# Attention units of two query heads, with score rows in pieces of 512 keys

## The chip, the cores and the metric

The kernel runs on one core of a Trainium2 chip. The metric is the device time of one execution in microseconds, taken as the median of three runs. The engines are TensorE (PE, with its weight loads as PEld), VectorE (DVE), ScalarE (ACT), GpSimd (POOL) and the queue SyncE (SP), which issues the transfers. Each engine works its own list of instructions in order, and waits where an instruction needs something that another engine has not finished.

## What is computed

The reference is a backbone of two layers over 2048 latent tokens and 256 context tokens of width 1024. The even layer has two groups of heads side by side, behind one input projection and ahead of one output projection: four heads of a bidirectional gated delta rule ("gdn"), and attention of four query heads over two heads of keys and values (2304 keys, 128 channels). The odd layer is a Conformer convolution module. The part that the change rewrites is the attention:

```python
def grouped_attend(q, k, v):
    bsz, nq = q.shape[:2]
    qg = q.reshape(bsz, nq, B_KV, B_HEADS // B_KV, B_HD)
    s = jnp.einsum('bqhgd,bnhd->bhgqn', qg, k).astype(F32) * (B_HD ** -0.5)
    p = jax.nn.softmax(s, axis=-1).astype(v.dtype)
    o = jnp.einsum('bhgqn,bnhd->bqhgd', p, v)
    return o.reshape(bsz, nq, B_HEADS * B_HD)
...
    k_all = jnp.concatenate([k_l, k_c], axis=1)
    v_all = jnp.concatenate([v_l, v_c], axis=1)
...
    yb_l = ob * jax.nn.silu(zb_l)
    out_l = jnp.concatenate([ya_l, yb_l.astype(ya_l.dtype)], axis=-1) @ w_out
```

The gated delta rule of the other heads runs over chunks. For each chunk it needs the inverse of a unit triangular matrix, and then a chain of small products that carries a state from chunk to chunk, once forward and once backward.

## The kernel before

Every product in float32 precision is made of three: an operand is split into a high part (hi) and a rest (lo), and hi x hi, hi x lo and lo x hi are summed in PSUM. `mm3` (L135 to L137) issues the three, `split` (L145, L146) makes the parts.

*Layer 0, input (`layer0_in`).* The projections write q, k, v, z and the gdn's operands to DRAM. In the last sections the triangular inverses of the gdn run beside projections: `gdn_subst` works by substitution on diagonal blocks of 32 (names sbC and sbT, two tiles of the pool `subst`). It takes five passes, one for each group of chunks. A pass loads its blocks (L836, L838, L839), then alternates 31 multiplications (L846, on DVE while small, on POOL when large) with 31 reductions on DVE (L847), copies (L849, ACT) and stores the inverses (L855). A generator emits the passes 2 to 4 beside the last projection, so the scheduler may let them run on into the next stage.

*Layer 0, mix (`layer0_mix`).* Two generators are merged: `attention` and `gdn_all`, at a ratio of 865 steps to 500. Gdn needs the inverses of the passes as they come: `gdn_inverse` (tiles psq, psw, pst) and `gdn_chain` (pk, py, pq, pn, pa).

The attention before takes 32 units of one head and 256 queries. A unit has two rows of 128 queries. For each row, `scores` makes five blocks of scores (ps_s, four of 512 keys and one of 256), copies them to tiles S of 1024 keys (the rest in S2 of 256) with their maximum (L1049, DVE), and then takes the exponential in place, three instructions a row (L1058, ACT). `attention` goes over the keys of a unit in nine steps of 256: four transposes (pt, L1091), the cast to phi (L1095, ACT), the rest plo (L1096, DVE), and then `pv`: six products with v of 256 moving columns into po (L1119, L1120, L1123). A plan of numbers says how many score blocks of the next unit are issued in each step. `load_kv_part` loads k and v of one kv head; the stage tile kvraw is an S tile, v is cast to vhi (DVE) and vlo (POOL).

*Layer 0, output.* Tokens in groups of 128 are multiplied by the output weight (ps_out), normed and added to the residual x, whose tiles (x1) are loaded ahead.

The order on each engine is not written by hand: a scheduler with its own timing model sets it from the order in which the generators emit, and from the dependences. Memory is part of these. Pools are stacks that grow from the left or from the right end of SBUF. A pool opened with `reuse_waits="tile"` may use addresses that an earlier, closed pool had, and each of its tiles then waits until the last use of the tiles that lie under it is done.

Of the kernel before, what the change touches and what calls it, by code (L numbers as in the profile page):

```python
# [8 lines left out]
F32 = mybir.dt.float32  # L9
# [22 lines left out]
GDN_STEPS = 500  # L32

# [73 lines left out]
class Build:  # L107
# [82 lines left out]
    def ada_start(self, layer, conds, half, raws, pspool, ap, st):  # L190
        """Scale and shift columns {cond: (A[128,4], B[128,4])} of four channel tiles."""
# [43 lines left out]
    def make_hT(self, xs, A, B, hi, lo, st, tp, cts=range(KT), bufs=3):  # L235
        """xs: token tiles [128,1024] scaled by rstd; writes hi/lo [128 ch, 8, n*128]."""
# [12 lines left out]
    @staticmethod  # L249
    def pipe(gens):  # L250
        """Starts one generator per tick, then each older one takes a step, newest first. A generator
        that is given more than once takes a single step each time."""
# [11 lines left out]
    def rotate(pools):  # L264
        """Allocator over four buffers of the first pool and two of the second, in turn."""
# [9 lines left out]
    def ahead(self, gen, offset, steps=2):  # L275
        """gen, its first steps with a scheduling priority that lies `offset` instructions earlier."""
        for _ in range(steps):
            with self.tc.high_priority(offset):
                next(gen)
            yield  # L280
        yield from gen

    def layer0_in(self):
        tc, nc = self.tc, self.nc
        with ExitStack() as es:
# [67 lines left out]
            with tc.tile_pool(name="stB", bufs=2, reuse_waits="tile") as st:  # L353
# [25 lines left out]
                self.pipe([late])  # L379
            with tc.tile_pool(name="stZ", bufs=2, reuse_waits="tile") as st:  # L380
                self.sub = em.enter_context(tc.tile_pool(name="subst", bufs=1, side="right", reuse_waits="tile"))
# [49 lines left out]
    def load_w(self, src, c0, n, vec=False):  # L431
        """Weight columns [1024, n] as hi/lo half tiles of four k tiles each."""
# [286 lines left out]
    # gated delta rule, chunks of 128 tokens, four heads at a time: first the decayed products of all  # L719
    # chunks and the inverses of their diagonal blocks of 32, then both directions' chains, where the  # L720
    # chain of a chunk runs beside the completion of the next one's inverse and the output of the last
# [95 lines left out]
    def gdn_subst(self, n, chunks):  # L817
        """Inverses of the unit triangular diagonal blocks of 32 of one group of chunks for each direction, by
# [695 lines left out]
```

## Time and profile before

| | |
|---|---|
| median of 3 runs | 2692.19 us (2688.54 to 2692.4) |
| profiled execution | span 2690.4 us, 1.8 us below the median |
| PE busy | 2595.6 us, 96% |
| DVE busy | 2027.2 us, 75% |
| ACT busy | 1357.0 us, 50% |
| POOL busy | 1427.6 us, 53% |
| attention stage | 882 to 1815 us of the span |
| first and last product with v | 912.9 and 1814.7 us |
| first and last reduction of the substitution | 671.0 and 1166.4 us |

In the rows of the profile a tile is written out<-in, with the buffer numbers left out, and "x" gives a count. Times are microseconds from the start of the span, or ns where the text says so. Busy time of PE holds waits as well where matmuls are pipelined, so what an operation costs on PE is read from the distance of two starts or from a window's sum.

### The profile page before, as it was taken

What the parts mean: (1) busy time and instruction counts of PE and PEld (TensorE: products, weight loads), DVE (VectorE), ACT (ScalarE), POOL (GpSimd) and SP (SyncE); (2) the same over time, 40 slices, a digit from 0 to 9 for tenths busy, and PEclk for the clock granted to TensorE, in tenths of its full rate; (3) what the DMA queues carried; (4) which work ended last, traced back from release to release, by engine and by line L of the source; (5) the groups of instructions that cost most, each with busy time, mean ns of one, the idle gap of its engine ahead of it and who ended that gap; (6) DMA issues with size and microseconds to landing.
All of it is one profiled execution on the core that took longest, in us unless ns stands there. A gap on an engine that the chain in (4) does not pass through costs nothing. (4 is left out here: it accounts for less than half of the span.)

```text
span 2690.4 us, 44112 instructions
## 1 busy us (share of the span) xinstructions
PE 2595.6 (96%) x15784; PEld 2235.1 (83%) x15784; DVE 2027.2 (75%) x4048; ACT 1357.0 (50%) x2617; POOL 1427.6 (53%) x1172
## 2 busy tenths in 40 slices
PE   7999999998899899999999999999999999999988
PEld 5888887998788688888888889888888888887867
DVE  8576667776975778776676667656379999997985
ACT  7454465223232555555555555544356767665332
POOL 3344343667776645431243332302169999997764
PEclk9999999999999999999999999999999999999999
DMA  8133334335556654444544433324411211116442
GB/s 308 50 103 101 116 118 130 111 114 147 178 170 199 167 116 109 130 115 120 148 124 122 117 103 97 112 85 135 155 49 40 71 57 62 55 59 202 159 155 98
DMA packets 372731, 323.28 MB, mean 120 GB/s; under 512 B 74784, under 2 KB 301600, under 8 KB 372512
## 3 DMA queue, kind: packets, MB, share of 16 engines
q1 hardware_dynamic: 372512, 320.46, 39.6%
q8 instruction: 125, 2.05, 0.3%
q14 instruction: 94, 0.77, 0.1%
HBM read 216.05 MB, written 104.33 MB: 119 GB/s over the span
## 5 line engine op out<-in xcount | busy, mean ns | idle before, releaser
L1392 POOL TENSOR_TENSOR ac<-ac,pr 128x512 f32<-128x512 f32 x288 | 379.3, 1340 | 22.1 <-ACT ac L1388 10.5
L1384 DVE SCALAR_TENSOR_TENSOR pc<-u,hw,pc 128x1024 f32<-128x1024 f32 x320 | 389.3, 1279 | 2.0 <-ACT pc L1382 0.7
L1095 ACT CAST phi<-pt 128x512 fp32r<-128x512 f32 x288 | 166.6, 586 | 217.5 <-PE pt L1091 207.3
L1391 ACT ACTIVATE pr<-u,hw 128x512 f32<-128x512 f32 x288 | 205.9, 722 | 124.1 <-POOL ac L1392 122.7
L1096 DVE TENSOR_TENSOR plo<-pt,phi 128x512 fp32r<-128x512 f32 x288 | 195.9, 685 | 84.1 <-ACT phi L1095 82.5
L1049 DVE TENSOR_SCALAR_CACHE_REDUCE S<-ps_s 128x512 f32<-128x512 f32 (+1 forms) x320 | 198.9, 631 | 63.3 <-PE ps_s L137 41.5
L135 PE MATMUL ps_b<-w_hi,hhi 128*128 128x256 f32 (+1 forms) x800 | 231.9, 292 | 7.3 <-DVE xn L563 5.8
L136 PE MATMUL ps_b<-w_lo,hhi 128*128 128x256 f32 (+1 forms) x800 | 228.4, 287 | 0.1
L137 PE MATMUL ps_b<-w_hi,hlo 128*128 128x256 f32 (+1 forms) x800 | 227.1, 289 | 0.6 <-POOL hlo L146 0.6
L135 PE MATMUL ps_out<-wohi,yhi 128*128 128x512 f32 x512 | 204.3, 399 | 2.2 <-DVE yhi L145 2.2
L137 PE MATMUL ps_out<-wohi,ylo 128*128 128x512 f32 x512 | 201.6, 395 | 0.6 <-DVE ylo L146 0.6
L136 PE MATMUL ps_out<-wolo,yhi 128*128 128x512 f32 x512 | 202.0, 395 | 0.0
L1058 ACT ACTIVATE S<-S,m 128x1024 f32<-128x1024 f32 (+1 forms) x192 | 177.9, 931 | 36.5 <-DVE m L1055 36.3
L846 POOL TENSOR_TENSOR sbT<-sbC 128x169 f32<-128x169 f32 (+18 forms) x76 | 122.1, 1607 | 103.9 <-DVE sbC L847 79.5
L1091 PE MATMUL pt<-ident,S 128*128 128x128 f32 x1152 | 175.5, 274 | 0.9 <-DVE plo L1096 0.9
L1119 PE MATMUL po<-phi,vhi 128*128 128x256 f32 x576 | 170.1, 317 | 3.8 <-ACT phi L1095 3.2
L135 PE MATMUL ps_a<-hhi,w_hi 128*128 128x512 f32 (+1 forms) x448 | 171.3, 382 | 0.0
L136 PE MATMUL ps_a<-hlo,w_hi 128*128 128x512 f32 (+1 forms) x448 | 170.8, 381 | 0.0
L137 PE MATMUL ps_a<-hhi,w_lo 128*128 128x512 f32 (+1 forms) x448 | 170.3, 380 | 0.2 <-POOL w_lo L146 0.2
L474 DVE SCALAR_TENSOR_TENSOR acc<-ub,cols,acc 128x512 f32<-128x512 f32 (+1 forms) x168 | 138.7, 834 | 33.8 <-POOL acc L472 32.0
L135 PEld LDWEIGHTS ps_b<-w_hi,hhi 128*128 128x128 f32 x800 | 153.9, 193 | 10.0 <-issue 4.8
L136 PEld LDWEIGHTS ps_b<-w_lo,hhi 128*128 128x128 f32 x800 | 154.0, 193 | 1.6 <-DVE w_lo L146 0.6
(323 smaller groups left out, 7699.2 us busy)
## 6 DMA issues: line engine op xcount, KB each, us to landing
raw_ada<-in_ada_w_dram SPq DMA_DIRECT2D x48, 512.0 KB
x<-in_x_dram SPq DMA_DIRECT2D x32, 512.0 KB
kq<-d_kT SPq DMA_DIRECT2D x54, 256.0 KB
raw_w<-in_ev_w_in_dram SPq DMA_DIRECT2D x26, 512.0 KB
kq<-d_qT SPq DMA_DIRECT2D x48, 256.0 KB
raw_w<-in_od_w_in_dram SPq DMA_DIRECT2D x24, 512.0 KB
d_nt<-ntA SPq DMA_DIRECT2D x36, 256.0 KB
nt<-d_nt SPq DMA_DIRECT2D x36, 256.0 KB
```

The costliest lines, as they stand in the source:

```text
L135: self.nc.tensor.matmul(ps, lhsT=lh, rhs=rh, start=(a == 0), stop=False)
L136: self.nc.tensor.matmul(ps, lhsT=lh, rhs=rl, start=False, stop=False)
L137: self.nc.tensor.matmul(ps, lhsT=ll, rhs=rh, start=False, stop=(a == n - 1))
L1049: nc.vector.tensor_scalar(out=S[g][:, k0:k0 + w], in0=ps[:, :w], scalar1=1.0, scalar2=None, op0=ALU.mult, op1=ALU.max, accum_out=mx[:, b:b ...
L1058: nc.scalar.activation(S[g], S[g], AF.Exp, bias=m, scale=scale, accum_out=l[:, g:g + 1])
L1091: nc.tensor.transpose(pt[:, e, a * P:(a + 1) * P], S[a][k0 // 1024][:, k0 % 1024:k0 % 1024 + P], self.ident)
L1095: nc.scalar.copy(hi, pt)
L1096: nc.vector.tensor_tensor(out=lo, in0=pt, in1=hi.bitcast(F32), op=ALU.subtract)
L1119: nc.tensor.matmul(po, lhsT=vhi[:, ks], rhs=hi[:, e, :], start=(k == 0), stop=False)
L1384: nc.vector.scalar_tensor_tensor(out=pc, in0=s(j), scalar=w(j), in1=pc, op0=ALU.mult, op1=ALU.add)
L1391: nc.scalar.mul(pr, s(j), w(j))
L1392: nc.gpsimd.tensor_tensor(out=ac, in0=ac, in1=pr, op=ALU.add)
```

## The change

A unit now is two heads of one kv head with 256 queries, four rows of 128; there are 16. Products have 512 moving columns, three to a step of 128 keys, with 18 steps. The score tiles are pieces of 512 keys (S_BUFS 20) and 256 keys (S2_BUFS 6), so a row has five exponentials. k and v are loaded in pieces of 512. The tiles qr, qhi, qlo and ya have one buffer instead of two and are twice as wide. The pool `subst` is opened on the left side, ahead of stZ and for the whole of `layer0_in`; before it was opened on the right side inside stZ, for the whole of the mix. Comments are removed, which is left out here.

```diff
+S_BUFS = 20
+S2_BUFS = 6
...
+            self.sub = es.enter_context(tc.tile_pool(name="subst", bufs=1, reuse_waits="tile"))
             with tc.tile_pool(name="stZ", bufs=2, reuse_waits="tile") as st:
-                self.sub = em.enter_context(tc.tile_pool(name="subst", bufs=1, side="right", reuse_waits="tile"))
                 with tc.tile_pool(name="prod", bufs=2, side="right", reuse_waits="tile") as gp:
                     prod = self.all_products(gp, self.tp)
...
-                stage = lambda w: self.ap.tile([P, w], F32, tag="S" if w > 256 else "S2", name="kvraw", bufs=7 if w > 256 else 4)
+                stage = lambda w: self.ap.tile([P, w], F32, tag="S" if w > 256 else "S2", name="kvraw", bufs=S_BUFS if w > 256 else S2_BUFS)
...
-        for k0, w in ((0, 1024), (1024, 1024), (2048, 256)):
+        for k0 in range(0, T + TC, 512):
+            w = min(512, T + TC - k0)
...
-    def scores(self, kv, h, qp, kvt):
-        """Yields after each of ten score blocks; the last value is the unit's state."""
+    def scores(self, kv, qp, kvt):
+
         nc, ap = self.nc, self.ap
         scale = float(P) ** -0.5
         khi, klo = kvt[0], kvt[1]
-        qr = ap.tile([P, 256], F32, tag="qr", name="qr", bufs=2)
-        nc.sync.dma_start(qr, self.d_bq[h, :, qp * 256:(qp + 1) * 256])
-        sz = ap.tile([P, 256], F32, tag="sz", name="sz", bufs=2)
-        nc.sync.dma_start(sz, self.d_szb[h, :, qp * 256:(qp + 1) * 256])
-        qhi = ap.tile([P, 256], F32R, tag="qhi", name="qhi", bufs=2)
-        qlo = ap.tile([P, 256], F32R, tag="qlo", name="qlo", bufs=2)
+        hs, ts = slice(2 * kv, 2 * kv + 2), slice(qp * 256, (qp + 1) * 256)
+        qr = ap.tile([P, 2, 256], F32, tag="qr", name="qr", bufs=1)
+        nc.sync.dma_start(qr, self.d_bq[hs, :, ts].rearrange("h p t -> p h t"))
+        sz = ap.tile([P, 2, 256], F32, tag="sz", name="sz", bufs=2)
+        nc.sync.dma_start(sz, self.d_szb[hs, :, ts].rearrange("h p t -> p h t"))
+        qhi = ap.tile([P, 2, 256], F32R, tag="qhi", name="qhi", bufs=1)
+        qlo = ap.tile([P, 2, 256], F32R, tag="qlo", name="qlo", bufs=1)
         self.split(qhi, qlo, qr)
-        st = {"S": [], "r": [], "sz": sz, "h": h, "qp": qp, "kv": kvt}
-        for a in range(2):
-            S = [None] * 3
+        st = {"S": [], "r": [], "sz": sz, "kv": kv, "qp": qp, "kvt": kvt}
+        for e, a in ((0, 0), (0, 1), (1, 0), (1, 1)):
+            S = []
             mx = ap.tile([P, 5], F32, tag="mx", name="mx")
             qs = slice(a * P, (a + 1) * P)
-            for b, (g, k0, w) in enumerate(self.KB):
-                if S[g] is None:
-                    S[g] = (ap.tile([P, 1024], F32, tag="S", name="S", bufs=7) if g < 2
-                            else ap.tile([P, 256], F32, tag="S2", name="S2", bufs=4))
+            for b in range(5):
+                w = 512 if b < 4 else 256
+                S.append(ap.tile([P, 512], F32, tag="S", name="S", bufs=S_BUFS) if b < 4
+                         else ap.tile([P, 256], F32, tag="S2", name="S2", bufs=S2_BUFS))
                 ps = self.ps_s.tile([P, 512], F32, tag="s", name="ps_s")
-                ks = slice(g * 1024 + k0, g * 1024 + k0 + w)
-                self.mm3(ps[:, :w], [(qhi[:, qs], qlo[:, qs], khi[:, ks], klo[:, ks])])
-                nc.vector.tensor_scalar(out=S[g][:, k0:k0 + w], in0=ps[:, :w], scalar1=1.0, scalar2=None,
+                ks = slice(b * 512, b * 512 + w)
+                self.mm3(ps[:, :w], [(qhi[:, e, qs], qlo[:, e, qs], khi[:, ks], klo[:, ks])])
+                nc.vector.tensor_scalar(out=S[b], in0=ps[:, :w], scalar1=1.0, scalar2=None,
                                         op0=ALU.mult, op1=ALU.max, accum_out=mx[:, b:b + 1])
                 if b < 4:
                     yield
             m = ap.tile([P, 1], F32, tag="m", name="m")
             nc.vector.reduce_max(m, mx, axis=AX.X)
             nc.vector.tensor_scalar(out=m, in0=m, scalar1=-scale, scalar2=None, op0=ALU.mult)
-            l = ap.tile([P, 3], F32, tag="l", name="l")
-            for g in range(3):
+            l = ap.tile([P, 5], F32, tag="l", name="l")
+            for g in range(5):
                 nc.scalar.activation(S[g], S[g], AF.Exp, bias=m, scale=scale, accum_out=l[:, g:g + 1])
-            ri = ap.tile([P, 1], F32, tag=f"ri{a}", name=f"ri{a}")
+            ri = ap.tile([P, 1], F32, tag=f"ri{e}{a}", name=f"ri{e}{a}")
             nc.vector.reduce_sum(ri, l, axis=AX.X)
             nc.vector.reciprocal(ri, ri)
             st["S"].append(S)
@@ -1065,16 +1067,14 @@
 
     def attention(self):
         nc, ap = self.nc, self.ap
-        units = [(kv, 2 * kv + hh, qp) for kv in range(KV) for qp in range(T // 256) for hh in range(2)]
-        gen = None
+        units = [(kv, qp) for kv in range(KV) for qp in range(T // 256)]
+        plan = (2, 1, 1, 1) * 4 + (0, 0)
+
+        def start(u):
+            return self.scores(*units[u], self.load_kv(units[u][0]))
+
+        gen = start(0)
         cur = None
-        plan = (2, 1, 2, 1, 2, 1, 1, 0, 0)
-
-        def start(u):
-            kv = units[u][0]
-            return self.scores(*units[u], self.load_kv(kv))
-
-        gen = start(0)
         for cur in gen:
             yield
         pend = None
@@ -1082,60 +1082,58 @@
             gen = start(u + 1) if u + 1 < len(units) else None
             nxt = None
             po = None
-            S, vhi, vlo = cur["S"], cur["kv"][2], cur["kv"][3]
-            for kp in range(NTA // 2):
-                pt = self.ps_t.tile([P, 2, 256], F32, tag="t", name="pt")
-                for e in range(2):
-                    for a in range(2):
-                        k0 = (2 * kp + e) * P
-                        nc.tensor.transpose(pt[:, e, a * P:(a + 1) * P], S[a][k0 // 1024][:, k0 % 1024:k0 % 1024 + P],
-                                            self.ident)
-                hi = ap.tile([P, 2, 256], F32R, tag="phi", name="phi", bufs=2)
-                lo = ap.tile([P, 2, 256], F32R, tag="plo", name="plo", bufs=2)
+            for k in range(NTA):
+                pt = self.ps_t.tile([P, 512], F32, tag="t", name="pt")
+                k0 = k * P
+                for a in range(4):
+                    nc.tensor.transpose(pt[:, a * P:(a + 1) * P], cur["S"][a][k0 // 512][:, k0 % 512:k0 % 512 + P],
+                                        self.ident)
+                hi = ap.tile([P, 512], F32R, tag="phi", name="phi", bufs=2)
+                lo = ap.tile([P, 512], F32R, tag="plo", name="plo", bufs=2)
                 nc.scalar.copy(hi, pt)
                 nc.vector.tensor_tensor(out=lo, in0=pt, in1=hi.bitcast(F32), op=ALU.subtract)
                 yield
                 if gen is not None:
-                    for _ in range(plan[kp]):
+                    for _ in range(plan[k]):
                         nxt = next(gen)
                     yield
                 if pend is not None:
                     pend()
                     yield
-                if kp == 0:
-                    po = self.ps_o.tile([P, 256], F32, tag="o", name="po")
-                pend = self.pv(po, vhi, vlo, hi, lo, kp, cur)
+                if k == 0:
+                    po = self.ps_o.tile([P, 512], F32, tag="o", name="po")
+                pend = self.pv(po, hi, lo, k, cur)
             cur = nxt
         pend()
         yield
 
-    def pv(self, po, vhi, vlo, hi, lo, kp, st):
+    def pv(self, po, hi, lo, k, st):
         nc, ap = self.nc, self.ap
+        vhi, vlo = st["kvt"][2:]
 
         def emit():
-            for e in range(2):
-                k = 2 * kp + e
-                ks = slice(k * P, (k + 1) * P)
-                nc.tensor.matmul(po, lhsT=vhi[:, ks], rhs=hi[:, e, :], start=(k == 0), stop=False)
-                nc.tensor.matmul(po, lhsT=vlo[:, ks], rhs=hi[:, e, :], start=False, stop=False)
-            for e in range(2):
-                k = 2 * kp + e
-                nc.tensor.matmul(po, lhsT=vhi[:, k * P:(k + 1) * P], rhs=lo[:, e, :], start=False, stop=(k == NTA - 1))
-            if kp == NTA // 2 - 2:
-                pr = self.ps_t.tile([P, 256], F32, tag="t", name="pr")
-                for a in range(2):
+            ks = slice(k * P, (k + 1) * P)
+            nc.tensor.matmul(po, lhsT=vhi[:, ks], rhs=hi, start=(k == 0), stop=False)
+            nc.tensor.matmul(po, lhsT=vlo[:, ks], rhs=hi, start=False, stop=False)
+            nc.tensor.matmul(po, lhsT=vhi[:, ks], rhs=lo, start=False, stop=(k == NTA - 1))
+            szf = st["sz"].rearrange("p h t -> p (h t)")
+            if k == NTA - 2:
+                pr = self.ps_t.tile([P, 512], F32, tag="t", name="pr")
+                for a in range(4):
                     nc.tensor.transpose(pr[:, a * P:(a + 1) * P], st["r"][a].to_broadcast([P, P]), self.ident)
-                nc.vector.tensor_tensor(out=st["sz"], in0=pr, in1=st["sz"], op=ALU.mult)
-            if kp == NTA // 2 - 1:
-                y = ap.tile([P, 256], F32, tag="ya", name="ya")
-                nc.vector.scalar_tensor_tensor(out=y, in0=po, scalar=0.5, in1=st["sz"], op0=ALU.mult, op1=ALU.mult)
-                nc.sync.dma_start(self.d_y[H + st["h"], :, st["qp"] * 256:(st["qp"] + 1) * 256], y)
+                nc.vector.tensor_tensor(out=szf, in0=pr, in1=szf, op=ALU.mult)
+            if k == NTA - 1:
+                y = ap.tile([P, 2, 256], F32, tag="ya", name="ya", bufs=1)
+                nc.vector.scalar_tensor_tensor(out=y.rearrange("p h t -> p (h t)"), in0=po, scalar=0.5, in1=szf,
+                                               op0=ALU.mult, op1=ALU.mult)
+                h0 = H + 2 * st["kv"]
+                nc.sync.dma_start(self.d_y[h0:h0 + 2, :, st["qp"] * 256:(st["qp"] + 1) * 256].rearrange("h p t -> p h t"), y)
 
         return emit
```

Three places where the order of the engines changes. A row is a line, an instruction, its tiles, its shape, and a count where rows alike follow each other.

First DVE, where v of the first kv head is cast (vhi<-kvraw). sbC<-sbT is a reduction of the substitution, whose last in the program has the shape 128x31; S,mx<-ps_s copies a score block; qz, r, o and sso belong to the gdn. Before:

```order
L847 TENSOR_REDUCE sbC<-sbT 128x16
L1049 TENSOR_SCALAR S,mx<-ps_s 128x512 x2
L1049 TENSOR_SCALAR S_10400,mx<-ps_s 128x256
L145 CAST vhi<-kvraw 128x1024 x2
L145 CAST vhi<-kvraw 128x256
L898 COPY qz_32_10298<-psq 32x4x32 x2
L1054 TENSOR_REDUCE m<-mx 128x1
L847 TENSOR_REDUCE sbC<-sbT 128x17
```

After:

```order
L849 TENSOR_REDUCE sbC<-sbT 128x30
L900 COPY qz_64_10313<-psq 64x256
L963 TENSOR_TENSOR S_16252<-S_16252,pn 128x512
L963 TENSOR_TENSOR S_16276<-S_16276,pn 128x512
L849 TENSOR_REDUCE sbC<-sbT 128x31
L971 TENSOR_TENSOR o<-o,pa 128x512 x2
L900 COPY qz_32_10307<-psq 32x4x32 x2
L900 COPY qz_32_10311<-psq 32x4x32 x2
L936 SCALAR_TENSOR_TENSOR r<-pk,negc,vt 128x128 x8
L987 TENSOR_REDUCE sso<-o_16438 128x4
L988 TENSOR_SCALAR sso<-sso 128x4
L147 CAST vhi<-kvraw 128x512 x4
```

The casts of v stood in the middle of the third pass of the substitution, and stand behind the last reduction of the fifth. On PE the first product with v moves with them: it was instruction 5101, 97 behind the first score matmul at 5004, and is 6105, 1101 behind it.

Then PE, where the last units of the attention meet the output projection (ps_out). Before, in one of the last units:

```order
L1123 MATMUL po<-plo,vhi 128x256 x2
L135 MATMUL ps_s<-khi,qhi 128x512
L136 MATMUL ps_s<-klo,qhi 128x512
L137 MATMUL ps_s<-khi,qlo 128x512
L1091 MATMUL pt<-ident,S 128x128 x4
L135 MATMUL ps_out<-wohi_21445,yhi 128x512
L136 MATMUL ps_out<-wolo_21446,yhi 128x512
L135 MATMUL ps_out<-wohi_21469,yhi 128x512
L136 MATMUL ps_out<-wolo_21470,yhi 128x512
L1119 MATMUL po<-phi,vhi 128x256
```

After, at the end of the last unit (pr are the transposes of the row sums):

```order
L1123 MATMUL pr<-ident,ri_20230 128x128
L1123 MATMUL pr<-ident,ri_20321 128x128
L1116 MATMUL po<-phi,vhi 128x512
L1117 MATMUL po<-phi,vlo 128x512
L1118 MATMUL po<-plo,vhi 128x512
L137 MATMUL ps_out<-wohi_20645,yhi 128x512
L138 MATMUL ps_out<-wolo_20646,yhi 128x512
L137 MATMUL ps_out<-wohi_20669,yhi 128x512
```

265 matmuls of ps_out stood among the attention's by the trace; now the first stands behind the last product with v.

Last ACT, in the part of the attention after the gdn, from the end of a unit (its last ten casts phi) into the next. S,l<-S,m are exponentials of the pieces of one row: four of 512 and one of 256. After:

```order
L1093 CAST phi<-pt 128x512 x10
L1060 ACTIVATE S,l<-S,m 128x512 x4
L1060 ACTIVATE S_14431,l<-S_14431,m 128x256
L1060 ACTIVATE S,l<-S,m 128x512 x4
L1060 ACTIVATE S_14574,l<-S_14574,m 128x256
L1093 CAST phi<-pt 128x512 x2
L1060 ACTIVATE S,l<-S,m 128x512 x4
L1060 ACTIVATE S_14813,l<-S_14813,m 128x256
L1093 CAST phi<-pt 128x512 x4
```

The exponentials of two whole rows stand between the last cast of a unit and the first of the next, at every one of the 15 boundaries (13 and 15 exponentials at two of them); before there were none to three at such a place.

More of the change, by code (lines that the diff above doesn't have):

```diff
@@ L998, in gdn_final @@
         yield
-    KB = [(0, 0, 512), (0, 512, 512), (1, 0, 512), (1, 512, 512), (2, 0, 256)]
     def load_kv(self, kv):
```

## The prediction

> **What bounds the kernel now.** The page first: TensorE is the busy engine.
>
> ```profile
> span 2690.4 us, 44112 instructions
> PE 2595.6 (96%) x15784; PEld 2235.1 (83%) x15784; DVE 2027.2 (75%) x4048; ACT 1357.0 (50%) x2617; POOL 1427.6 (53%) x1172
> ```
>
> Then the table by windows, cut at the stage that the change touches: 882 us (first scores) to 1815 us (last product with v). Columns: window, its length, busy time (count) of PE, PEld, DVE, ACT, POOL, then granted clock, DMA share, GB/s.
>
> ```profile
> 882.00:1150.00 268.00, 256.16 (x1986) 222.15 (x1985) 214.28 (x603) 146.32 (x318) 141.88 (x120) 0.98 0.51 132
> 1150.00:1655.00 505.00, 502.34 (x3937) 447.21 (x3936) 346.06 (x975) 277.11 (x626) 158.71 (x146) 1.00 0.42 115
> 1660.00:1680.00 20.00, 19.47 (x141) 17.68 (x140) 14.04 (x44) 12.21 (x26) 7.21 (x7) 1.00 0.42 139
> 1680.00:1700.00 20.00, 17.25 (x116) 15.27 (x115) 13.14 (x41) 15.30 (x28) 9.55 (x5) 0.97 0.54 161
> 1700.00:1720.00 20.00, 19.98 (x128) 18.04 (x127) 16.28 (x43) 15.18 (x26) 9.56 (x4) 0.94 0.45 132
> 1720.00:1815.00 95.00, 95.00 (x552) 83.37 (x552) 51.93 (x117) 40.11 (x79) 5.00 (x10) 1.00 0.24 79
> ```
>
> PE is full in all but the first and the fourth, so here a transfer or a DVE operation costs only if PE runs out of work. The same windows for tile po (products with v), then pk (one step of the gdn chain), then ps_out (the output projection of layer 0):
>
> ```profile
> 1150.00:1655.00 505.00, 178.93 (x958) 134.13 (x956) 7.61 (x18) 1.00 0.42 115
> 1660.00:1680.00 20.00, 9.62 (x55) 7.94 (x56) 0.42 (x1) 1.00 0.42 139
> 1680.00:1700.00 20.00, 9.06 (x50) 7.42 (x51) 0.42 (x1) 0.97 0.54 161
> 1700.00:1720.00 20.00, 9.53 (x52) 7.95 (x50) 0.42 (x1) 0.94 0.45 132
> ...
> 882.00:1150.00 268.00, 11.72 (x80) 10.47 (x81) 11.18 (x40) 0.98 0.51 132
> 1150.00:1655.00 505.00, 28.23 (x192) 25.43 (x192) 27.19 (x96) 1.00 0.42 115
> ...
> 1700.00:1720.00 20.00, 2.99 (x12) 2.28 (x13) 0.00 (x0) 0.00 (x0) 0.94 0.45 132
> 1720.00:1815.00 95.00, 62.44 (x253) 46.13 (x252) 13.31 (x20) 7.25 (x21) 1.00 0.24 79
> ```
>
> Three streams share PE until 1815: attention, gdn, and 265 matmuls of ps_out. I price them per record. Attention without gdn, its scores and transposes included, costs (20 + 20 - 12 x 0.23)/(55 + 52) = 0.35 us per po record in the third and fifth windows (0.36 and 0.33 apart; 0.40 in the fourth). So 1728 products stand for 605 us. In 1150 to 1655 the rest is gdn: (505 - 958 x 0.35)/192 = 0.88 per pk record, 240 us for 272. The 265 of ps_out are 61. That is 906 of 933 us; 12 of the rest are idle in the first window.
>
> **The products.** 1728 matmuls of 256 columns become 864 of 512. Pitches, start to start, from the timeline of PE:
>
> ```profile
> 882.88 0.39 PE L136 MATMUL ps_s<-klo,qhi 128*128 128x512 f32 x1
> 883.11 0.39 PE L137 MATMUL ps_s<-khi,qlo 128*128 128x512 f32 x1
> ...
> 1225.06 0.28 PE L1120 MATMUL po<-phi,vlo 128*128 128x256 f32 x1
> 1225.17 0.28 PE L1119 MATMUL po<-phi,vhi 128*128 128x256 f32 x1
> ...
> 1370.93 0.82 PE L1091 MATMUL pt<-ident,S 128*128 128x128 f32 x6
> ```
>
> 0.23 against 0.1175 (0.11 and 0.12 alternate): 203.0 us becomes 198.7, a gain of 4.3 us. The Trainium skill ("TensorE: Matmul & The Clock Gate", section "Back-to-back issue gap") gives columns over 2.4 GHz plus 2.5 ns: 109 and 216 ns, which is an estimate of 2 us saved. The rows lie above both, so I keep 4.3. Transposes (six in 0.82 us, 0.11 each when the last one's 0.27 is taken off) and score matmuls keep their number.
>
> **Score rows in pieces.** Per row four exps of 512 replace two of 1024:
>
> ```profile
> L1058 ACT ACTIVATE S<-S,m 128x1024 f32<-128x1024 f32 x128 | 146.4, 1147 | 36.5 <-DVE m L1055 36.3
> L1058 ACT ACTIVATE S<-S,m 128x256 f32<-128x256 f32 x64 | 31.9, 498 | 0.0
> L1095 ACT CAST phi<-pt 128x512 fp32r<-128x512 f32 x288 | 166.6, 586 | 217.5 <-PE pt L1091 207.3
> L1096 DVE TENSOR_TENSOR plo<-pt,phi 128x512 fp32r<-128x512 f32 x288 | 195.9, 685 | 84.1 <-ACT phi L1095 82.5
> ```
>
> On the line between the two widths 512 columns take about 0.71 us (an estimate from these rows; 0.50 and 1.15 are its ends). 256 x 0.71 - 146.4 is 36 us more on ACT, and each exp brings an accumulator read. ACT is 55% busy in the second window and its casts wait for PE (207.3 us), so the total hides. Where the exps stand does not: a unit now has four rows and the pool S2 six buffers, so the last pieces of the next unit's third and fourth rows wait for this unit's last transposes. In the order on ACT ten exps stand between each unit's last phi and the next one's first; before, none to three. That chain is phi 0.59 + plo 0.69 + exps 8 x 0.71 + 2 x 0.50 = 6.7 + phi 0.59 = 8.5 us; PE has six products (1.4), eight score blocks of three matmuls (six of 512 and two of 256 columns, 4.8) and twelve transposes (1.3) there, 7.5. Gdn fills the first boundaries; for ten I take 1 us each, +10, with ends 0 and 60 (6 us each, if the score blocks must wait for DVE too).
>
> **The moved pool.** This decides. The tiles sbC and sbT of the substitution move from the right side, inside stZ, to the left before it; in the program as built they then share addresses with vhi and vlo of kv head 0 (sbT 190016 to 194112, vhi 184256 to 193472), and a pool that reuses memory waits for its last user. Before they shared none:
>
> ```profile
> L1119 PE MATMUL po<-phi,vhi x576: 274/283/561, 912.9 to 1814.3; 128*128 128x256 f32 x192
> L145 DVE CAST vhi<-kvraw x6: 679/1192/2464, 894.8 to 1370.1; 128x1024 fp32r<-128x1024 f32 x4, 128x256 fp32r<-128x256 f32 x2
> L146 POOL TENSOR_TENSOR vlo<-kvraw,vhi x6: 734/2391/2818, 896.0 to 1375.8; 128x1024 fp32r<-128x1024 f32 x4, 128x256 fp32r<-128x256 f32 x2
> ```
>
> v was cast at 895 and the first product ran at 912.9, long before the substitution ended. Its five passes end in the copies L849 (the first at 757):
>
> ```profile
> 848.70 2.12 ACT L849 COPY sbT<-sbC 128x1024 f32<-128x1024 f32 x1 [4.90 <-DVE sbC L847]
> ...
> 969.47 2.01 ACT L849 COPY sbT<-sbC 128x1024 f32<-128x1024 f32 x1
> ...
> 1065.06 2.08 ACT L849 COPY sbT<-sbC 128x1024 f32<-128x1024 f32 x1 [1.05 <-DVE sbC L847]
> ...
> 1167.60 2.05 ACT L849 COPY sbT<-sbC 128x1024 f32<-128x1024 f32 x1 [1.13 <-DVE sbC L847]
> ...
> L847 DVE TENSOR_REDUCE sbC<-sbT x155: 136/414/1156, 671.0 to 1166.4; 128x1 f32<-128x1 f32 x4, 128x2 f32<-128x4 f32 x4, 128x3 f32<-128x9 f32 x4, 128x4 f32<-128x16 f32 x4
> L846 POOL TENSOR_TENSOR sbT<-sbC x76: 637/1565/3030, 786.5 to 1162.9; 128x169 f32<-128x169 f32 x4, 128x196 f32<-128x196 f32 x4, 128x225 f32<-128x225 f32 x4, 128x256 f32<-128x256 f32 x4
> ```
>
> The lengths are 121, 96 and 103 us. The third pass lost 12 us between two groups of its loads, with v's loads among what stood there on SP; these now stand behind:
>
> ```profile
> 858.48 1.96 SPq L836 DMA_DIRECT2D sbT<-d_nt  x4
> ...
> 870.46 2.42 SPq L836 DMA_DIRECT2D sbT<-d_nt  x4
> ...
> 1174.65 1.81 SPq L855 DMA_DIRECT2D d_w<-sbC  x4
> ```
>
> Its own work bounds a pass below: 19 POOL multiplies at 1.57 and 31 reductions at 0.41, alternating, are 43 us, with loads, small multiplies, copies and stores some 66. Without products fewer plo stand on DVE between its steps, but more gdn operations on DVE and POOL; I take 105, 94 and 93. The last copy then starts at 848.7 + 292 = 1141, its store ends 8 us after (1174.65 + 1.81 - 1167.60 = 8.9 in the row), and v is cast: first product at about 1150. Its ends: 1069 and 1185 (lengths as before, plus stores and casts); 1069 is set by PE, as the next lines show, since three passes of 66 would end sooner, at 1056.
>
> Until then the order on PE holds 96 of the 136 pk matmuls (71% of gdn, 170 us; the trace has two records of each) and 81 of 960 score matmuls (17 us): 187 us of work in 268, so 81 us idle. From 1150 on: 29% of gdn, 70 us; attention 605 - 4 - 17 = 584; boundaries 10; the second head's v (casts around 1370, vlo 2.4 us each) with less gdn to cover it, 6 (ends 0 and 12). The sum is 670: attention ends at 1820.
>
> **What it covered.** The first residual tile of layer 0's output (x1) shared addresses with the substitution before, and shares them now with klo, which the last scores use. The order on PE has no ps_out before the last po; before there were 265. So 61 us follow alone, and about 3 us of start: 1820 + 64 = 1884 where the kernel before stood at 1815. That is +69; behind it nothing changes. From the profiled span 2690.4 it gives 2759, and the median lies 1.8 above that span: **2761 us**. DMA issues of the larger q, sz and ya are half as many and twice as large; q is split for 512 columns at once, DVE is 69% busy in the second window and does that beside PE: nothing.
>
> **The rivals.**
>
> *The substitution runs much faster alone.* The loss is gone when the first product comes 69 us earlier, at 1081, so when a pass takes 74 us: 848.7 + 3 x 74 + 9. Shorter ones gain no more than PE's own 187 us allow, a first product at 1069 and 2680 us. For it: attention was beside every pass after the second. Against: the second pass, mostly without attention, still took 848.7 - 757 = 92 us. Chance 0.08, half of it below 2687 and half on no change.
>
> *Attention alone is slower than I price it.* The fourth window shows 0.40 per record while ACT was 15.30 of 20 us busy. At 0.40 the attention costs 86 us more, and gdn by the same division 0.63 instead of 0.88, 20 us less at the end: +66, 2827. With boundaries of 6 us it goes the same way. Chance 0.12.
>
> *PE runs at half speed while it waits.* After an idle time the pitch was not 0.23:
>
> ```profile
> 890.91 0.77 PE L135 MATMUL ps_s<-khi,qhi 128*128 128x512 f32 x1 [6.72 <-DVE S L1049]
> 891.48 0.63 PE L136 MATMUL ps_s<-klo,qhi 128*128 128x512 f32 x1
> 891.91 0.63 PE L137 MATMUL ps_s<-khi,qlo 128*128 128x512 f32 x1
> ```
>
> 891.48 to 891.91 is 0.43. If the gaps before the first product keep PE in that state, its 187 us there become up to 374 in 268, and the first product slips by up to 106: up to 2867. If only gaps of several us do it, the 80 us of slack hide it. The Trainium skill has this rule (same page, section "Why this matters for your kernels"): a gap of over about 3 us brings the array back to half rate. The row agrees after 6.7 us; none here shows many small gaps. Chance 0.06.
>
> *The wait is not there.* Then only the products (-4) and the boundaries (0 to 10) count, and 2688 to 2698 follows. The order speaks against it: v's casts stand behind the last reduction on DVE. Chance 0.02.
>
> **The numbers.** The forecast, first product between 1105 and 1185, has 0.72: 2715 to 2800. With the second rival and part of the third the range is 2705 to 2830. A measurement here tells about 0.2%, 5 us, from no change. Faster 0.04; same 0.04 and the last rival, 0.06; slower 0.90.
>
> **What would show it.** First product near 1150 and v's casts right behind the last sbC reduction; PE busy about 0.7 from 890 to then; last product near 1820 with no ps_out before; products at a pitch of 0.23; ACT casts waiting for exps at unit boundaries. Wrong, if the substitution ends before 1080, if PE stays full until then, or if the last product comes after 1880.

## The result, and the profile after

The changed kernel takes 2787.69 us (median of four runs, 2784.1 to 2796.48) against 2692.3 before, a ratio of 1.0362 [1.0345, 1.0379]: 95 us slower, where 2761 was forecast, with a range to 2830. Its profiled execution is the slowest of the four, 104.3 us longer in its span than the one before. The first lines of its page:

```profile
span 2794.7 us, 42560 instructions
PE 2612.8 (93%) x14920; PEld 2188.2 (78%) x14920; DVE 2045.9 (73%) x3992; ACT 1395.4 (50%) x2875; POOL 1423.4 (51%) x1178
```

PE has 864 matmuls less and is busy 17 us longer, in a span of which it fills 93% and not 96%. The windows show where (columns as before), then the same for pk:

```profile
882.00:1150.00 268.00, 221.22 (x1957) 193.34 (x1956) 159.01 (x424) 112.93 (x308) 188.56 (x173) 0.92 0.79 217
1162.00:1400.00 238.00, 232.94 (x1586) 192.40 (x1587) 162.88 (x439) 139.67 (x360) 96.27 (x90) 0.98 0.39 113
1400.00:1600.00 200.00, 178.55 (x920) 140.03 (x918) 139.06 (x374) 117.41 (x276) 31.71 (x18) 0.93 0.17 52
1600.00:1820.00 220.00, 208.51 (x1132) 166.01 (x1130) 161.37 (x462) 137.18 (x341) 0.00 (x0) 1.00 0.09 26
...
882.00:1150.00 268.00, 24.77 (x176) 22.33 (x176) 24.09 (x88) 0.92 0.79 217
1162.00:1400.00 238.00, 11.50 (x80) 10.63 (x80) 11.19 (x40) 0.98 0.39 113
```

Before 1150 PE works on gdn (176 of its 272 pk records, 80 before) and on little else, the first unit's scores, and idles 47 us; after 1400, where POOL and the DMA fall quiet, it works on attention alone and idles again. The tile v and the ends of the substitution's passes, from the view by tile and the timeline of ACT, with DVE's and SP's rows at the turning point:

```profile
L1116 PE MATMUL po<-phi,vhi x288: 389/476/793, 1162.3 to 1848.7; 128*128 128x512 f32 x144
L147 DVE CAST vhi<-kvraw x10: 419/1370/1524, 1161.8 to 1554.2; 128x512 fp32r<-128x512 f32 x8, 128x256 fp32r<-128x256 f32 x2
...
857.69 2.12 ACT L851 COPY sbT<-sbC 128x1024 f32<-128x1024 f32 x1 [4.84 <-DVE sbC L849]
955.76 1.96 ACT L851 COPY sbT<-sbC 128x1024 f32<-128x1024 f32 x1 [3.60 <-DVE sbC L849]
1054.18 1.99 ACT L851 COPY sbT<-sbC 128x1024 f32<-128x1024 f32 x1
1151.12 2.01 ACT L851 COPY sbT<-sbC 128x1024 f32<-128x1024 f32 x1 [1.54 <-DVE sbC L849]
...
1158.18 1.81 SPq L857 DMA_DIRECT2D d_w<-sbC  x4
...
1161.78 2.20 DVE L147 CAST vhi<-kvraw 128x512 fp32r<-128x512 f32 x3 [4.56 <-DMA d_w<-sbC]
```

v's casts wait for the last store of the substitution (released by d_w<-sbC), and the first product with v follows at 1162.3, where it stood at 912.9.

How PE's time is spent from the first score matmul to the last product, added up from the traces (start of a matmul to the start of the next; idle is the time from a matmul's end to the next start; waits inside the pitch count to the stream), all in us:

| kernel | first score | first product | last product | attention | gdn | ps_out | idle | from last product to the end |
|---|---|---|---|---|---|---|---|---|
| before | 882.6 | 912.9 | 1814.7 | 599.7 | 253.2 | 61.4 | 17.8 | 875.7 |
| changed | 891.7 | 1162.3 | 1849.3 | 591.6 | 271.9 | 0 | 94.0 | 945.4 |
| b_left | 884.4 | 1175.4 | 1875.1 | 578.1 | 269.2 | 49.1 | 94.2 | 883.2 |
| b_pad | 883.5 | 914.6 | 1752.4 | 602.0 | 248.6 | 0 | 18.4 | 937.1 |
| r16 | 879.9 | 924.2 | 1806.1 | 612.9 | 262.0 | 0 | 51.3 | 940.0 |
| r20g | 883.2 | 928.4 | 1783.2 | 606.4 | 259.2 | 0 | 34.4 | 939.4 |
| s18 | 887.0 | 1183.8 | 1936.2 | 586.4 | 271.0 | 66.5 | 125.4 | 876.8 |

Changed against before: 76 us more idle, 19 more in gdn, 8 less in attention, 9 later at the first score, and ps_out, which leaves the stage (-61) and comes behind it (+70): 104.

### The profile page after: what moved, and what is told of

It is laid out like the page before. It is cut to its first block, busy times and chain, and to the rows that moved or that the text cites. A ratio compares the mean times of both kernels' runs of the same rounds, so it can differ in the third digit from the quotient of the medians.

```text
span 2794.7 us, 42560 instructions
## 1 busy us (share of the span) xinstructions
PE 2612.8 (93%) x14920; PEld 2188.2 (78%) x14920; DVE 2045.9 (73%) x3992; ACT 1395.4 (50%) x2875; POOL 1423.4 (51%) x1178
## 5 line engine op out<-in xcount | busy, mean ns | idle before, releaser
L1060 ACT ACTIVATE S<-S,m 128x512 f32<-128x512 f32 (+1 forms) x320 | 213.2, 669 | 32.5 <-DVE m L1057 30.2
L151 POOL TENSOR_TENSOR rsp<-msp,mhalf 128x1 f32<-128x1 f32 x32 | 19.0, 594 | 405.7 <-DVE msp L1217 405.7
L1089 PE MATMUL pt<-ident,S 128*128 128x128 f32 x1152 | 181.7, 277 | 9.1 <-ACT S L1060 9.1
L1089 PEld LDWEIGHTS pt<-ident,S 128*128 128x128 f32 x1152 | 146.7, 143 | 45.8 <-ACT S L1060 10.4
L137 PE MATMUL ps_s<-khi,qhi 128*128 128x512 f32 (+1 forms) x320 | 139.4, 436 | 25.0 <-DVE S L1051 23.6
```

What stands on the lines that cost most here:

```text
L137: self.nc.tensor.matmul(ps, lhsT=lh, rhs=rh, start=(a == 0), stop=False)
L1060: nc.scalar.activation(S[g], S[g], AF.Exp, bias=m, scale=scale, accum_out=l[:, g:g + 1])
L1089: nc.tensor.transpose(pt[:, a * P:(a + 1) * P], cur["S"][a][k0 // 512][:, k0 % 512:k0 % 512 + P], self.ident)
```

## The experiments

Two theories after the result. **Pool**: sharing addresses with the substitution holds v back, and that idle time is the loss. **Units**: the rewritten units with their order of scores and exps lose the time themselves.

**b_left: the pool alone.**

```diff
--- before
+            self.sub = es.enter_context(tc.tile_pool(name="subst", bufs=1, reuse_waits="tile"))
             with tc.tile_pool(name="stZ", bufs=2, reuse_waits="tile") as st:
-                self.sub = em.enter_context(tc.tile_pool(name="subst", bufs=1, side="right", reuse_waits="tile"))
```

> The kernel before, with one edit: the pool of the substitution (sbC, sbT) is opened on the left, as in the changed kernel; units, score pieces and buffers stay. If the pool's place carries the loss: v of kv head 0 waits for the end of the substitution, first product with v near 1155 us instead of 913, PE busy about 0.7 until then, and some 84 us more minus what ps_out fills later (211 of its matmuls still stand ahead of the last product), so 2755 to 2780 us. If the loss lies in the new units and score pieces: first product near 913 and 2692 us, within 5.

2768.95 us, ratio 1.0287 [1.0259, 1.0315]. With the old units and score pieces the first product comes at 1175.4, and 78 us are lost. The idle time is in sum that of the changed kernel (94 us), but not in the same places: 81 us of it lie ahead of the first product and 13 behind it, against 51 and 43 in the changed kernel. A window ahead of the first product shows how little PE has to do, and at what granted clock (0.77):

```profile
1050.00:1150.00 100.00, 53.61 (x490) 48.25 (x489) 41.41 (x103) 29.25 (x74) 63.45 (x56) 0.77 0.59 156
```

**b_pad: the left side without the shared addresses.**

```diff
--- b_left
+            pad = pool("pad", 1, side="right")
+            pad.tile([P, 4192], F32, name="pad")
             self.vv = pool("vv", 1, side="right")
```

> As b_left (kernel before, pool of the substitution on the left), with 16768 bytes left empty between k and v, so that v of kv head 0 lies below the substitution's tiles. The score tiles then reach down onto the output stage's work tiles, and no ps_out stands ahead of the last product (211 in b_left, 264 before). If sharing addresses with v is what costs: first product back near 913 us, and 2690 to 2705 us, since PE has hardly an idle time that ps_out could fill. If the left side costs for another reason: about 2769, as b_left. If ps_out behind the last product is a loss of its own: 2750.

2693.39 us, ratio 1.0006 [0.9992, 1.0020]. The rows of v in b_left, then in b_pad:

```profile
L145 DVE CAST vhi<-kvraw x6: 685/693/2445, 1174.6 to 1551.9; 128x1024 fp32r<-128x1024 f32 x4, 128x256 fp32r<-128x256 f32 x2
...
L1121 PE MATMUL po<-phi,vhi x576: 274/283/389, 914.6 to 1751.8; 128*128 128x256 f32 x192
L145 DVE CAST vhi<-kvraw x6: 282/688/2460, 875.6 to 1369.4; 128x1024 fp32r<-128x1024 f32 x4, 128x256 fp32r<-128x256 f32 x2
```

The pool is still on the left; v only lies elsewhere, and everything is back. It also settles ps_out: none stands ahead of the last product here, the stage is 63 us shorter and what follows 61 us longer. Its place is no loss while PE is full.

**r16 and r20g: the new units alone.** Both put the pool back on the right in the changed kernel, and pay the 8 KB in different places.

```diff
--- changed (r16)
-S_BUFS = 20
+S_BUFS = 16
-            self.sub = es.enter_context(tc.tile_pool(name="subst", bufs=1, reuse_waits="tile"))
             with tc.tile_pool(name="stZ", bufs=2, reuse_waits="tile") as st:
+                self.sub = em.enter_context(tc.tile_pool(name="subst", bufs=1, side="right", reuse_waits="tile"))
--- changed (r20g): the same move of the pool, S_BUFS stays 20
-        kq = self.load_kq(c, gp, 4)
+        kq = self.load_kq(c, gp, 3)
-            at = gp.tile([P, H, P], F32, tag="at", name="at", bufs=4)
+            at = gp.tile([P, H, P], F32, tag="at", name="at", bufs=3)
-        o = gp.tile([P, H, P], F32, tag="o", name="o", bufs=4) if lat else None
+        o = gp.tile([P, H, P], F32, tag="o", name="o", bufs=3) if lat else None
```

> The changed kernel with the pool of the substitution back on the right side (needs 8 KB: S_BUFS 16 instead of 20, so a unit's score pieces have no spare buffers). If the pool's place carries the loss: first product near 915 us, and the 84 us that PE lost before it are back: about 2704 us (2690 to 2720); ps_out still stands behind the last product. If the new units carry it: 2770 us or more, since units and exps are as in the changed kernel.

> As r16 (pool on the right) with all 20 score buffers; the 8 KB come from the gdn's buffers (kq, at and o three instead of four). If the short stock of 16 score buffers makes r16's units slow (40.5 us against 37.1 without gdn beside them): units of 37 us, first product 10 us earlier than r16's 924, and 2720 to 2735 us. If units of two heads cost that much with any stock: 2751, as r16. If the gdn with three buffers becomes late: above 2751.

r16: 2750.84 us, ratio 1.0223 [1.0206, 1.0240]. The first product is back at 924, but only 37 of 95 us are regained; neither number I had given was met. r20g: 2724.46, 1.0111 [1.0088, 1.0134], in the band of the short stock; but its first product stands at 928.4, not 10 us ahead of r16's. Attention without gdn beside it, 100 us of r16, r20g and b_left:

```profile
1660.00:1760.00 100.00, 88.98 (x463) 69.84 (x463) 67.30 (x191) 58.38 (x145) 0.00 (x0) 0.97 0.06 20
...
1650.00:1750.00 100.00, 93.89 (x503) 73.70 (x504) 70.82 (x198) 62.85 (x148) 11.94 (x5) 1.00 0.15 45
...
1700.00:1800.00 100.00, 100.00 (x706) 90.43 (x706) 79.95 (x239) 58.78 (x119) 0.00 (x0) 1.00 0.06 20
```

Old units fill PE there, new ones do not. From the starts of ya (one a unit): 40.5 us a unit in r16, 36.9 to 37.1 in r20g and the changed kernel, and 34.6 for two old units in b_left. So of the 57 us by which r16 exceeds b_pad, 26 go with the stock of 16 score buffers for units that need 16 (r16 less r20g, which also has fewer buffers for gdn). The other 30 are the units with a stock of 20: against b_pad, r20g has 16 us more idle, 11 more in gdn and 4 more in attention. That gdn has three buffers there is not what makes it longer: r16, with four, shows 262.0 us. Both theories hold, and their losses (78 and 30 us) together exceed the 95. One reason is in the traces: the last three passes of the substitution take 315 us in b_left and 293 in the changed kernel, so there the first product comes 20 us sooner after the first score. Why the passes differ is open.

**s18: the score tiles off the output stage's work tiles.**

```diff
--- changed
-S_BUFS = 20
+S_BUFS = 18
```

> The changed kernel with S_BUFS 18 instead of 20, which moves the lowest score tile from address 116224 to 120320, off the small work tiles of the output stage (ss2, junk, msp, rs and others, 116000 to 118276); x1 stays where it was, over klo. 276 matmuls of ps_out then stand ahead of the last product instead of none. If these tiles, not x1, keep ps_out back, and ps_out only fills time in which PE waits: 2743 to 2768 us. If the 61 us of ps_out behind the last product are a loss of their own: 2718. If x1 over klo is what counts on the chip: 2788, no change. First product near 1160 in all three.

2811.63 us, 1.0448 [1.0425, 1.0471]: 24 us slower than the changed kernel, which no theory had. ps_out did come forward (66.5 us of it in the stage, 68.6 less behind it), so it neither gained nor lost. The loss is ahead of it, at the first product. DVE, ACT and PE of s18 there:

```profile
1170.41 4.87 DVE L147 CAST vhi<-kvraw 128x512 fp32r<-128x512 f32 x5 [5.34 <-DMA d_w<-sbC]
...
1179.85 0.72 ACT L1060 ACTIVATE S<-S,m 128x512 f32<-128x512 f32 x1 [4.06 <-DVE m L1057]
...
1183.80 0.50 PE L1116 MATMUL po<-phi,vhi 128*128 128x512 f32 x1 [0.68 <-ACT phi L1093]
```

v's stage tiles kvraw hold four score buffers until v is cast. 20 buffers leave 16, the first unit's need; 18 leave 14, so its last row is finished only after the cast: 13.4 us from the cast to the first product, 0.5 in the changed kernel (1161.8 and 1162.3). The other 8.6 us lie ahead of the cast; the last three passes of the substitution take 307 us here, 293 there.

**r16q: the same for r16.**

```diff
--- r16
-                y = ap.tile([P, 2, 256], F32, tag="ya", name="ya", bufs=1)
+                y = ap.tile([P, 2, 256], F32, tag="qr", name="ya", bufs=1)
-            mx = ap.tile([P, 5], F32, tag="mx", name="mx")
+            mx = ap.tile([P, 6], F32, tag="mx", name="mx")
-            m = ap.tile([P, 1], F32, tag="m", name="m")
-            nc.vector.reduce_max(m, mx, axis=AX.X)
+            m = mx[:, 5:6]
+            nc.vector.reduce_max(m, mx[:, 0:5], axis=AX.X)
```

> As r16 (pool on the right, 16 score buffers of 512), with ya in the tile of qr and the row maximum in mx's tile, 2 KB less, so that the score tiles lie above the output stage's work tiles; 360 matmuls of ps_out then stand ahead of the last product instead of none. If ps_out only fills time in which PE waits (s18 against the changed kernel: last product later by the ps_out it took in, end 3 us apart once the later first product is taken off): 2735 to 2750 us, at most the 20 us of gaps at the last five boundaries below r16's 2751. If ps_out behind the last product is a loss of its own: 2690.

2766.74 us, 1.0267 [1.0248, 1.0286]: slower than r16 by 16, which neither case had, though 86 us of ps_out moved into the stage. It did not fill the gaps (idle 58 us, 51 in r16). Which of its edits costs that is open.

**s17x8 and s20x8: the boundary.**

```diff
--- changed (s17x8)
-S_BUFS = 20
-S2_BUFS = 6
+S_BUFS = 17
+S2_BUFS = 8
--- changed (s20x8), with ya in qr's tile as in r16q
-S2_BUFS = 6
+S2_BUFS = 8
```

> As s18 (same addresses for the score tiles' low end), with S2_BUFS 8 and S_BUFS 17: the next unit's four last pieces no longer wait for this unit's last transposes, and the exps between two units' casts fall from ten to five or none. By the forecast's 1 us for each of ten boundaries: 5 to 15 us less than s18. If a boundary costs 3 us or more: 40 us less. If the work that now stands beside (ps_out, scores) covers the boundaries: the same as s18 within 5.

> The changed kernel with S2_BUFS 8 instead of 6 and 20 score buffers as there (ya shares qr's tile, so the memory is the same). The exps between two units' casts fall from ten to five or fewer. The changed kernel's units without gdn take 37.1 us, 1.9 of it idle on PE, and two of the old units in b_left 34.6. If the ten exps make that difference: 34.6 to 35.5 a unit, 15 to 25 us less in all, so 2763 to 2773. If it is the small stock of score buffers (20 for units of 16): 37 a unit and 2788, no change.

s17x8 takes 2815.59 us (1.0459 [1.0444, 1.0475]), as s18; but it has a score buffer less than s18, and 15.5 us from the cast of v to the first product. The cleaner s20x8 takes 2782.12 (1.0337 [1.0311, 1.0362]), an interval that overlaps the changed kernel's, and its units 37.0 us, with five exps or fewer at each of its 15 boundaries. So taking half of the ten exps away does not shorten a unit, though they stand there as forecast. The first exp, the tenth and the next cast on ACT in the changed kernel:

```profile
1671.21 0.73 ACT L1060 ACTIVATE S<-S,m 128x512 f32<-128x512 f32 x1 [0.82 <-DVE m L1057]
...
1677.37 0.49 ACT L1060 ACTIVATE S<-S,m 128x256 f32<-128x256 f32 x1
...
1677.86 1.04 ACT L1093 CAST phi<-pt 128x512 fp32r<-128x512 f32 x2
```

On what PE waits in such a unit, the view by tile of ps_s tells, here from 1640 to 1760 us: the idle time of the engines ahead of score work (PE and its weight loads counted apart), by what ended it, and how often, in the changed kernel and then in b_left:

```profile
  DVE S L1051: 16.9, 31
  PE pt L1089: 12.4, 7
...
  PE pt L1091: 4.4, 11
...
  DVE S L1049: 0.2, 1
```

Score blocks wait on PE until DVE has emptied a PSUM buffer (ps_s has two). In a steady unit this happens four times: 0.56 and 0.30 us at the boundary, where eight blocks stand close together, and 0.47 and 0.46 us some 4 and 13 us later, where DVE itself waits 1.6 and 2.0 us for transposes to free a score tile. That is read from the waits; no run took it away. In s20x8 the same line reads 7.0 instead of 16.9, waits for phi and plo stand beside it, and the units are as long: the wait moved, so which resource sets the 37 us is open. The stock of score buffers counts in any case: units without gdn and ps_out beside them take 40.5 us with 16, 38.4 with 18 (s18) and 37.1 with 20; no run had more than 20.

From the first to the last product of the changed kernel (1162.3 to 1849 us), the waits of PE that cost most are these (sum, times, longest):

```profile
PE ps_s L137 <- DVE S L1051: 16.8, 36, 1.1
PE po L1116 <- ACT phi L1093: 11.2, 5, 4.6
PE pt L1089 <- ACT S L1060: 9.1, 4, 4.2
```

The second and third end with an exp, or with a phi cast that stands behind exps on ACT. So the exps do hold PE, not in the steady units, but in a few long gaps: at the boundary with 13 of them (4.6 us, to 1440), at the last one (5.4 us, from 1821 to 1827), and at the two boundaries where the casts of the second head's k and v keep DVE from the row maximum that the exps need.

**u1024 and b512p: the score pieces.** u1024 is the changed kernel with 10 buffers of 1024 keys and three exps a row, b512p the kernel before with 14 of 512 and five.

```diff
--- changed (u1024; the exps, l and the transposes follow)
-S_BUFS = 20
+S_BUFS = 10
-                S.append(ap.tile([P, 512], F32, tag="S", name="S", bufs=S_BUFS) if b < 4
-                         else ap.tile([P, 256], F32, tag="S2", name="S2", bufs=S2_BUFS))
+                if b % 2 == 0:
+                    S.append(ap.tile([P, 1024], F32, tag="S", name="S", bufs=S_BUFS) if b < 4
+                             else ap.tile([P, 256], F32, tag="S2", name="S2", bufs=S2_BUFS))
--- before (b512p; likewise)
-                if S[g] is None:
-                    S[g] = (ap.tile([P, 1024], F32, tag="S", name="S", bufs=7) if g < 2
-                            else ap.tile([P, 256], F32, tag="S2", name="S2", bufs=4))
+                S.append(ap.tile([P, 512], F32, tag="S", name="S", bufs=14) if g < 2
+                         else ap.tile([P, 256], F32, tag="S2", name="S2", bufs=4))
```

> The changed kernel with the score pieces of before: 10 buffers of 1024 keys instead of 20 of 512, three exps a row, k and v loaded in 1024s; units of two heads and the pool on the left stay. If pieces of 512 cost by their added exps and accumulator reads: faster units than 37.1 us, and 10 to 25 us less than 2788. If pieces of 512 help because a piece comes free after four steps and not eight: slower units (39 to 42) and 2800 to 2850.

> The kernel before with only the score rows in pieces of 512 keys (14 buffers instead of 7 of 1024, five exps a row instead of three, k and v loaded in 512s); units, products and pools as before. If ACT's added 60 us hide, as the forecast says: 2692 us within 6. If the added exps stand in PE's way: 2700 to 2715.

u1024: 2794.74 us, 1.0376 [1.0354, 1.0397], units of 37.7 us: neither case came true, and with two-head units the size of the pieces hardly matters. b512p: 2701.04, 1.0045 [1.0026, 1.0063]: 10 us slower, so in the old units the smaller pieces do not quite hide. The run changes the exps and the pieces of k and v together, and its profiled execution, the fastest of its seven runs (2694.5), does not show which of them it is.

## Why the prediction came out as it did

- **First product: right.** Forecast 1150 from a first score at 882.6, so 267 us after it; measured 271. The three passes took 98, 98 and 97 us (from the copies' rows), 293 together, where I had 105, 94 and 93. They took 315 in b_left and 307 in s18, so a hit this close is partly luck. b_left and b_pad show the cause, which the prediction had only from addresses and order.
- **PE until then: right in kind.** 187 us of work were forecast in that time, 220 were spent (195 on gdn): the same matmuls took longer at the lower clock and with waits between them. It cost nothing, since the substitution set the end. The rival of half speed has this as its true part. The granted clock averaged 0.92 in this window and 0.77 in b_left's, and short windows show it at 0.50 behind idle times (rows in the last section). The Trainium skill ("TensorE: Matmul & The Clock Gate", section "Why this matters for your kernels") has the array fall to half rate after idle gaps of over about 3 us. The traces agree behind the gap of 4.6 us, but show the fall also behind gaps of 0.7 and 1.5 us that follow each other.
- **From first to last product: 687 us, forecast 670.** Attention took 567 after the first product, where 584 were forecast; the rest of gdn 77, not 70; but idle time was 43, where the boundaries (10) and the second v (6) stood for 16. That these errors partly cancel is luck. Attention without gdn was priced too high: two old units take 34.6 us in b_left, 0.32 for each of their 108 products, not 0.35, so the rival of slow attention is out. The step that was mis-sized is the boundary. Of the 43 us of idle time, 11 lie where k and v of the second head are cast, 5 at the boundary with 13 exps, 5 at the last one, and 12 in the units from 1600 to 1820, about 2 a unit. I took the ten exps as the chain; they took 6.65 us (1671.21 to 1677.86), 6.7 forecast, and s20x8 halved them for nothing. The end I had put at 6 us, "if the score blocks must wait for DVE too", names the wait of the steady units: such a unit is 2.5 us longer than two old ones, not 1. The exps themselves hold PE only in the few long gaps.
- **Exps on ACT "hide": wrong by up to 10 us** in the old units (b512p, which changes the pieces of k and v too), not separable in the new ones (u1024).
- **The products' 4.3 us: not to be seen in the total.** Two starts of 512-column products lie 0.23 us apart, as forecast, and the products alone take 244.9 us in r20g, with v in time, and 247.6 in b_pad; but attention as a whole is 4 us longer in r20g, not shorter.
- **ps_out behind the last product: the fact right, the reason wrong.** I put it down to x1 over klo. s18 left x1 where it was and moved the score tiles off the output stage's small work tiles, and ps_out came forward; r16q moved them likewise, with the same effect. And it was never a loss: in the sum it stood on both sides, and b_pad shows 0.06% without it.
- **Not foreseen:** 9 us ahead of the stage. Up to there both programs have the same order, but the end of the first pass of the substitution lies between 753 and 765 us over these kernels' profiles, so it differs by run; the median run of the changed kernel is 8.8 us shorter than its profiled one. And 6 us of start behind the last product beyond the 3 I gave.

From a profile of this length the terms were 9 + 3 + 17 + 6 = 35 us short of the profiled execution, 27 short of the median.

A version that beats both was not found. What the wider products can gain here is the 4.3 us of their pitch, 0.27 a unit, and a new unit without gdn beside it is 2.5 us longer than two old ones; the fastest kernel with the new units, r20g, is 1.1% slower than before.

## What to carry to other kernels

Where pools reuse each other's memory, read the addresses of the built program together with the order: a pool that moves to make room for buffers can lay an early operand under a late user, and no line of the diff says so. Price it as work that PE has left to do before the operand comes, against the time until then; work that changes its place while PE is full costs nothing. A larger unit needs its whole stock of tiles plus what other loads hold of the same ring: buffers that are missing show at the first unit (13.4 us in s18) and again in every later one (40.5, 38.4 and 37.1 us with 16, 18 and 20).

## What was not expected of the hardware

The granted clock changes within a few us, and its averages hide that. In b_left's window, which averaged 0.77, PE was not half busy throughout: it stood still from 1060 to 1080 and from 1130 to 1140 us; the clock averaged 0.58 in both, and 0.50 in the ten us behind each. In the changed kernel two gaps and the windows behind them, then a long window without such a gap:

```profile
1440.39 0.79 PE L1116 MATMUL po<-phi,vhi 128*128 128x512 f32 x1 [4.63 <-ACT phi L1093]
1439.00:1445.60 6.60, 5.21 (x16) 4.26 (x17) 3.48 (x8) 4.15 (x12) 1.17 (x1) 0.50 0.00 0
...
1510.82 0.50 PE L138 MATMUL ps_s<-klo,qhi 128*128 128x512 f32 x1 [0.65 <-POOL klo L148]
1512.81 0.50 PE L139 MATMUL ps_s<-khi,qlo 128*128 128x512 f32 x1 [1.49 <-DVE qlo L148]
1514.10:1524.10 10.00, 6.30 (x19) 4.78 (x20) 4.43 (x15) 5.54 (x14) 1.95 (x2) 0.50 0.35 105
...
1565.30:1824.50 259.20, 243.17 (x1320) 193.46 (x1318) 188.33 (x540) 160.52 (x400) 0.00 (x0) 1.00 0.09 27
```

Here the clock of 0.50 follows idle time that is dense within a few us, whether in one gap or in several (PE was busy 1.46 of the 3.2 us before 1513.9), and lasts 7 to 10 us. From 1600 to 1820, where PE idles 5 of 100 us in pieces of about half a microsecond, the clock stays at 1.00.
